# The layout of h in an fp32 decoder trunk: rows every 2048 bytes, and another layout for rows without the norm

## The chip, the core and the metric

The kernel runs on one NeuronCore of a Trainium2 chip. Its engines work side by side, each on its own stream of instructions: TensorE (PE: matmuls, and PEld, the weight loads that overlap them), VectorE (DVE), ScalarE (ACT), GpSimd (POOL) and SyncE (SP, which issues the DMAs). SBUF is the on-chip memory, 128 partitions wide; matmuls add up in the eight banks of PSUM. The metric is the device time of one execution in microseconds (us).

## What is computed

A trunk of two layers over 256 tokens and a width of 2048, all in float32. Layer 0 mixes tokens by retention, layer 1 by a short gated convolution; each is followed by a SwiGLU feed-forward of width 5632. A conditioning vector gives every sub-layer a shift, a scale and a gate.

```python
c_act = jax.nn.silu(c)
for i in range(DEPTH):
    mod = (c_act @ w_mod[i] + b_mod[i])[:, None, :]
    sh1, sc1, g1, sh2, sc2, g2 = jnp.split(mod, 6, axis=-1)
    h = (rms_norm(x, norm1_g[i]) * (1.0 + sc1) + sh1).astype(x.dtype)
    ...
    x = (x + g1 * y).astype(x.dtype)
    h = (rms_norm(x, norm2_g[i]) * (1.0 + sc2) + sh2).astype(x.dtype)
    x = (x + g2 * swiglu(h, ffn_w_in[i], ffn_w_out[i])).astype(x.dtype)
return rms_norm(x, final_g).astype(x.dtype)
```

## The kernel before, in words

Everything is kept transposed: a tile has 128 features on the partitions and the 256 tokens along the row. The 2048 features make KT = 16 such tiles, which the document calls rows: row j of h holds the features 128 j to 128 j + 127.

Precision: a float32 number is split into a high part, rounded to the type that TensorE takes in one pass (F32R), and a low part, the rest. A product is then high x high + high x low + low x high. A row of h is therefore 512 numbers in each partition: 256 of high, then 256 of low.

Weights come from HBM in one long array in the order of their use, in pieces of 128 x 2048 (`fetch`, a DMA on SP's queue, tile `raw`). `prepare` makes `hi` (L313, ScalarE) and `lo` (L316, VectorE) out of half a piece, 128 x 1024, that is eight blocks of 128 x 128. `take` hands them out one block after another.

Three functions multiply:

- `product` (L358, L361): per block one matmul of `hi` with the 512 columns of a row (high and low at once) and one of `lo` with its first 256. In it the row streams past the weights. It serves the feed-forwards and the convolution over h (3296 blocks), and the output products over `mid` (1604) and, in the retention, over tiles of the pool `rm` (496). `mid` and `rm` tiles have the shape of a row of h, 2048 bytes, each a tile of its own.
- `packed` (L398 to L400): three matmuls of 256 columns a block; for q, k and the gate in the retention, and for the last column of an output product.
- `by_token` (L373 to L375): for values v, whose tokens are to be on the partitions: here h is the stationary operand, 128 x 128, and 512 columns of weights stream.

The order is: the start (c, x and the scale and shift of layer 0 are made, first row groups of the retention's projection, up to about 190 us), the eight heads with the retention's output product, the first feed-forward in two halves (products over h, then an output product over `mid`), the convolution (over h, then its output), the second feed-forward, the last norm.

The order of TensorE's instructions, and in the start those of VectorE and ScalarE, is written by hand. The other engines' instructions are placed by a scheduler when their operands are ready.

Between two sub-layers TensorE would have to wait for the norm, a sum over all of x. The kernel avoids this: while the output product still finishes its columns, `scaled_only` (L487 to L494) writes x times the scale, without norm and without shift, into the rows of h. `normed` (L496) then multiplies these rows with the first six columns of the next weights (the first group, six PSUM banks), while the norm is worked out beside it. The norm is a factor for each token, so it can be applied to the result. The shift is not: it is multiplied as two tokens more, `ends`, whose high and low parts stand in front of a row's high part, so that two of its three matmuls take 258 columns (L519, L521) and one takes 256 (L520). Behind row k of these, `more` writes the finished rows of h (`modulated`: L465, L472, L473), at most up to row k - 1. All further groups read the finished rows.

The pools follow each other in memory: constants, work tiles, the weights' `raw`, `hi` and `lo`, then `hpool` with h, then what the retention and later the feed-forwards use (`rm`, `mid` and more). The tile `aside` of LEFT = 8 numbers stands in front of h. Row j of h begins MARGIN = 32 numbers behind the start of a stretch of 544 numbers; the two tokens of the shift are the last two of the margin.

## Time and profile before

| | before |
|---|---|
| median of 3 runs (lowest to highest) | 2639.91 us (2639.05 to 2640.29) |
| the profiled execution: its time, its span | 2639.47 us, 2637.7 us |
| mean granted TensorE clock in it | 0.998 |
| read from HBM | 682.99 MB, 260 GB/s over the span |
| DMA of the weights, w_all | 456 x 1024 KB |

How to read the lines of the profile that follow. In a group of instructions stand the source line, the engine, the operation, output<-inputs by the program's names, partitions x elements, the count, the busy time in us, the mean duration of one in ns, and the engine's idle time just before them with what ended it. A line of waits names who waited, for whom, the sum in us, how often, and the longest. In the view of one source line stand the durations (least/median/greatest, ns) and the start of the first and of the last in us. A row of stretches has the stretch, its length, the busy time and count of each engine (PE, PEld, DVE, ACT, POOL), the granted clock, the DMA engines' share and GB/s. In the timeline and in the chain of waits a row begins with its start and its length in us.

### The profile page before, as it was taken

Reading aid. Unit: us, or ns where it says so; the run is one execution under the profiler, and the core shown is the slowest. Engines: PE = TensorE matmul, PEld = TensorE weight load, DVE = VectorE, ACT = ScalarE, POOL = GpSimd, SP = SyncE. Lnnn points to the kernel's source line nnn. Section 1 sums busy time; section 2 is a strip of 40 time slices with the busy share of each in tenths; the row PEclk is TensorE's granted clock in tenths of the full one; section 3 lists DMA queues with packets and bytes.
Section 4 is the critical chain, followed back from the end, with each engine's and each line's share of the span. In section 5 each row is a group of like instructions: output and inputs, shape, how many; then the busy total and the mean of one; then the engine's idle time right before and its main releaser. Section 6 shows DMA issues by size and latency. Waiting matters only on the chain.

```text
span 2637.7 us, 38238 instructions
## 1 busy us (share of the span) xinstructions
PE 2604.2 (99%) x15220; PEld 2299.1 (87%) x15220; DVE 1989.0 (75%) x2527; ACT 1249.3 (47%) x1788; POOL 151.3 (6%) x230
## 2 busy tenths in 40 slices
PE   7999999999999999999999999999999999999998
PEld 5888889888899888888888898888988888888887
DVE  7898878777698877777777888888886665555564
ACT  5544443444456444344444454444554443444443
POOL 0000001110000011110100001100000000000000
PEclk9999999999999999999999999999999999999999
DMA  9977668777686877777777768777777665555553
GB/s 399 386 276 256 244 246 302 273 264 275 237 309 249 314 280 276 273 285 287 280 267 283 271 228 319 284 279 263 256 273 265 248 220 191 192 191 184 186 190 128
DMA packets 96950, 687.58 MB, mean 261 GB/s; under 512 B 10753, under 2 KB 12545, under 8 KB 13825
## 3 DMA queue, kind: packets, MB, share of 16 engines
q1 hardware_dynamic: 96770, 685.13, 70.8%
q8 instruction: 119, 1.95, 0.3%
q14 instruction: 61, 0.50, 0.1%
HBM read 682.99 MB, written 2.10 MB: 260 GB/s over the span
## 4 chain that ended last, share of the span: by engine, by line
PE 75%; issue 20%; DVE 2%; DMA 2%; ACT 1%; POOL 0%; DVEq 0%; ACTq 0%; POOLq 0%
PE bank L358 34%; PE bank L361 18%; PE bank L374 4%; PE bank L375 4%; PE bank L373 4%; PE bank L400 2%; PE bank L398 2%; PE bank L399 2%; PE bank L519 1%; PE bank L521 1%; PE bank L520 1%; DMA raw<-w_mod 1%; DVE raw L647 1%; DMA raw<-w_all 1%; DVE lo L316 1%
## 5 line engine op out<-in xcount | busy, mean ns | idle before, releaser
L316 DVE TENSOR_TENSOR lo<-raw,hi 128x1024 fp32r<-128x1024 f32 x912 | 1111.8, 1223 | 543.9 <-ACT hi L313 541.2
L313 ACT CAST hi<-raw 128x1024 fp32r<-128x1024 f32 x912 | 953.2, 1050 | 1073.9 <-PE bank L358 623.2
L358 PE MATMUL bank<-h,hi 128*128 128x512 f32 x3296 | 1153.8, 394 | 0.0
L361 PE MATMUL bank<-h,lo 128*128 128x256 f32 x3296 | 926.4, 281 | 0.0
L358 PEld LDWEIGHTS bank<-h,hi 128*128 128x128 f32 x3296 | 617.9, 187 | 140.0
L361 PEld LDWEIGHTS bank<-h,lo 128*128 128x128 f32 x3296 | 624.5, 189 | 0.0
L358 PE MATMUL bank<-mid,hi 128*128 128x512 f32 x1604 | 556.3, 390 | 0.0
L361 PE MATMUL bank<-mid,lo 128*128 128x256 f32 x1604 | 452.5, 282 | 1.1 <-DVE lo L316 1.1
L247 DVE SCALAR_TENSOR_TENSOR raw<-raw,cb 128x2048 f32<-128x2048 f32 x160 | 365.5, 2285 | 21.4 <-DMA raw<-w_mod 20.9
L358 PEld LDWEIGHTS bank<-mid,hi 128*128 128x128 f32 x1604 | 301.1, 188 | 63.0
L361 PEld LDWEIGHTS bank<-mid,lo 128*128 128x128 f32 x1604 | 303.4, 189 | 1.5 <-DVE lo L316 1.5
L374 PE MATMUL bank<-lo,h 128*128 128x512 f32 x512 | 203.3, 397 | 0.2 <-DVE lo L316 0.2
L373 PE MATMUL bank<-hi,h 128*128 128x512 f32 x512 | 203.4, 397 | 0.0
L375 PE MATMUL bank<-hi,h 128*128 128x512 f32 x512 | 203.2, 397 | 0.0
L358 PE MATMUL bank<-rm,hi 128*128 128x512 f32 x496 | 172.5, 391 | 0.0
L400 PE MATMUL bank<-h,lo 128*128 128x256 f32 x512 | 144.9, 283 | 9.2 <-DVE lo L316 9.2
L398 PE MATMUL bank<-h,hi 128*128 128x256 f32 x512 | 144.7, 283 | 2.5 <-ACT h L675 2.5
L399 PE MATMUL bank<-h,hi 128*128 128x256 f32 x512 | 144.4, 282 | 0.5 <-DVE h L676 0.5
L361 PE MATMUL bank<-rm,lo 128*128 128x256 f32 x496 | 139.9, 282 | 0.0
L375 PEld LDWEIGHTS bank<-hi,h 128*128 128x128 f32 x512 | 96.6, 189 | 23.3
L374 PEld LDWEIGHTS bank<-lo,h 128*128 128x128 f32 x512 | 96.5, 189 | 20.7 <-DVE lo L316 0.6
L373 PEld LDWEIGHTS bank<-hi,h 128*128 128x128 f32 x512 | 96.6, 189 | 20.2
(154 smaller groups left out, 2242.1 us busy)
## 6 DMA issues: line engine op xcount, KB each, us to landing
raw<-w_all SPq DMA_DIRECT2D x456, 1024.0 KB, 4.8
raw<-w_mod SPq DMA_DIRECT2D x192, 1024.0 KB, 5.0
x<-x_in SPq DMA_DIRECT2D x4, 512.0 KB, 5.6
out<-out SPq DMA_DIRECT2D x5, 256.0 KB, 3.4
decay<-tab_in SPq DMA_DIRECT2D x8, 128.0 KB, 2.2
out<-out SPq DMA_DIRECT2D x3, 128.0 KB, 2.5
out<-out SPq DMA_DIRECT2D x1, 384.0 KB, 2.7
cols<-cols_in SPq DMA_DIRECT2D x1, 160.0 KB, 8.7
```

Source lines behind the costliest of these rows:

```text
L247: nc.vector.scalar_tensor_tensor(raw, raw, 1.0, cb, op0=ALU.mult, op1=ALU.mult, accum_out=total)
L313: nc.scalar.copy(hi, raw)
L316: nc.vector.tensor_tensor(lo, raw, hi.bitcast(F32), op=ALU.subtract)
L358: nc.tensor.matmul(pt, hi, h, start=fresh and k == g.ks[0], stop=False, skip_group_check=True)
L361: nc.tensor.matmul(pt[:, 1, :], lo, h[:, 0, :], start=False, stop=last and k == g.ks[-1], skip_group_check=True)
L373: nc.tensor.matmul(o, ht[:, 0, :], hi, start=first, stop=False)
L374: nc.tensor.matmul(o, ht[:, 0, :], lo, start=False, stop=False)
L375: nc.tensor.matmul(o, ht[:, 1, :], hi, start=False, stop=last)
L398: nc.tensor.matmul(pt, hi, h[:, 0, :], start=first, stop=False, skip_group_check=True)
L399: nc.tensor.matmul(pt, hi, h[:, 1, :], start=False, stop=False, skip_group_check=True)
L400: nc.tensor.matmul(pt, lo, h[:, 0, :], start=False, stop=last, skip_group_check=True)
L519: nc.tensor.matmul(pt, hi, high, start=k == 0, stop=False, skip_group_check=True)
```

## The change

The margin goes. h becomes one stretch of 16 x 514 numbers, and two layouts are laid over it. The finished row j is the numbers 512 j to 512 j + 511 (`h`). The row without the norm is the numbers 514 j to 514 j + 513 (`raw_all`): first the two tokens of the shift, then 256 of high, then 256 of low. `scaled_only` and the matmuls of `normed` use the second, all else the first. A tile `beside` of 96 numbers, which nothing uses, is taken behind h. What lies behind it begins 1536 bytes lower than before. Line numbers from L485 on move by up to two.

```diff
-LEFT, MARGIN = 8, 32
+LEFT, ENDS = 8, 2
...
     hpool.tile([P, LEFT], F32, tag="aside", name="aside")
-    h_all = hpool.tile([P, KT, MARGIN + 2 * S], F32R, tag="h", name="h")
-    h = [h_all[:, j, MARGIN:].rearrange("p (a b) -> p a b", a=2) for j in range(KT)]
+    h_all = hpool.tile([P, KT * (ENDS + 2 * S)], F32R, tag="h", name="h")
+    hpool.tile([P, P - KT * ENDS], F32, tag="beside", name="beside")
+    h = [h_all[:, 2 * S * j : 2 * S * (j + 1)].rearrange("p (a b) -> p a b", a=2) for j in range(KT)]
+    raw_all = h_all.rearrange("p (k n) -> p k n", k=KT)
 
     def scaled_only(layer, norm, j):
 
         needed(layer, SC2 if norm else SC1, j)
         a = mod_a[layer][norm][:, j : j + 1]
-        nc.scalar.activation(h[j][:, 0, :], x[j], AF.Identity, scale=a)
-        nc.vector.scalar_tensor_tensor(
-            h[j][:, 1, :], x[j], a, h[j][:, 0, :].bitcast(F32), op0=ALU.mult, op1=ALU.subtract
-        )
+        high, low = raw_all[:, j, ENDS : ENDS + S], raw_all[:, j, ENDS + S :]
+        nc.scalar.activation(high, x[j], AF.Identity, scale=a)
+        nc.vector.scalar_tensor_tensor(low, x[j], a, high.bitcast(F32), op0=ALU.mult, op1=ALU.subtract)
...
-        ends = [h_all[:, :, MARGIN - 2 + i : MARGIN - 1 + i] for i in range(2)]
+        ends = [raw_all[:, :, i : i + 1] for i in range(ENDS)]
...
-            high, low = h_all[:, k, MARGIN - 2 : MARGIN + S], h[k][:, 1, :]
+            high, low = raw_all[:, k, : ENDS + S], raw_all[:, k, ENDS + S :]
```

## The prediction

> **What bounds the kernel now.** I read the page first: busy shares, then the groups of instructions.

> ```profile
> PE 2604.2 (99%) x15220; PEld 2299.1 (87%) x15220; DVE 1989.0 (75%) x2527; ACT 1249.3 (47%) x1788; POOL 151.3 (6%) x230
> ...
> L358 PE MATMUL bank<-h,hi 128*128 128x512 f32 x3296 | 1153.8, 394 | 0.0
> L361 PE MATMUL bank<-h,lo 128*128 128x256 f32 x3296 | 926.4, 281 | 0.0
> ...
> L358 PE MATMUL bank<-mid,hi 128*128 128x512 f32 x1604 | 556.3, 390 | 0.0
> ```

> TensorE is busy for 99% of the span. [...] Next I read who TensorE waited for after the first 190 us:

> ```profile
> PE bank L361 <- DVE lo L316: 1.1, 1, 1.1
> PE bank L455 <- POOL rs L448: 1.0, 1, 1.0
> PE bank L434 <- ACT acc L422: 0.9, 1, 0.9
> PE bank L874 <- DVE sp L416: 0.5, 1, 0.5
> PE bank L874 <- ACT sp L415: 0.3, 1, 0.3
> PE bank L374 <- DVE lo L316: 0.2, 1, 0.2
> ```

> That is 4 us in 2448 us. So the end is set by how fast TensorE takes its own stream, and a change of data layout matters only if it changes that pace. I therefore read the pace of the same code, `product`, from the view of one source line (count, durations, first and last start), in two stretches where it reads h and two where it reads mid:

> ```profile
> L358 PE MATMUL bank<-h,hi x704: 389/392/402, 1155.9 to 1401.9; 128*128 128x512 f32 x176
> ...
> L358 PE MATMUL bank<-h,hi x703: 390/392/402, 2255.5 to 2501.2; 128*128 128x512 f32 x176
> ...
> L358 PE MATMUL bank<-mid,hi x349: 389/390/391, 1034.2 to 1154.9; 128*128 128x512 f32 x175
> ...
> L358 PE MATMUL bank<-mid,hi x330: 389/390/394, 2501.9 to 2615.9; 128*128 128x512 f32 x165
> ```

> One block is a 512-column matmul and a 256-column one. With h it takes 246.0/703 = 349.9 and 245.7/702 = 350.0 ns; with mid 120.7/348 = 346.8 and 114.0/329 = 346.5 ns. The page says the same: 1153.8/3296 = 350.1 against 556.3/1604 = 346.8. The instructions and the weights' buffers are the same; what differs is where the moving rows lie. In the built program mid's rows follow each other every 2048 bytes, all 384 bytes past a multiple of 512. h's rows come every 2176 bytes, so each lies 128 bytes further within 512 than the one before, and the fourth comes round. The timeline of one such column shows that period (start, duration):

> ```profile
> 1284.34 0.40 PE L358 MATMUL bank<-h,hi 128*128 128x512 f32 x1
> ...
> 1284.70 0.39 PE L358 MATMUL bank<-h,hi 128*128 128x512 f32 x1
> ...
> 1285.74 0.40 PE L358 MATMUL bank<-h,hi 128*128 128x512 f32 x1
> ...
> 1287.14 0.40 PE L358 MATMUL bank<-h,hi 128*128 128x512 f32 x1
> ```

> The long one returns after 1.40 us, which is four blocks of 350 ns, and never with mid, whose longest is 391 or 394 ns.

> **The change part by part.** (1) *product over h.* After it h's rows come every 2048 bytes from byte 117632 of a partition, which is 384 past a multiple of 512: mid's places exactly. mid, rm and all that is allocated behind h move down by 1536 bytes, three times 512, and keep theirs. So I price the 3296 blocks at mid's pace: 3296 x (350.0 - 346.7) = 10.9 us off. Bounds: 346.8 and 346.5 give 10.5 and 11.5; zero if the row's place is not the cause.

> [...]

> (2) *packed over h* (L398 to L400, three 256-column matmuls a block). It runs over h in the retention stage and, on other tiles, at the ends of the output products:

> ```profile
> L398 PE MATMUL bank<-h,hi x63: 279/280/283, 433.2 to 455.2; 128*128 128x256 f32 x63
> ...
> L398 PE MATMUL bank<-mid,hi x15: 277/280/281, 1880.0 to 1884.9; 128*128 128x256 f32 x15
> ```

> 22.0/62 = 355 against 4.9/14 = 350 ns a block, and 512 blocks over h make 2.6 us. Of them 216 run in the first 190 us, where some of it is lost in waits for lo:

> ```profile
> PE bank L400 <- DVE lo L316: 7.6, 5, 2.2
> ```

> I take 2.2 us off, bounds 0 and 2.6.

> (3) *by_token* (L373 to L375). h is the stationary side here, the weights move. Six matmuls use one row of h, then six the next:

> ```profile
> L374 PE MATMUL bank<-lo,h x32: 392/395/397, 576.7 to 598.4; 128*128 128x512 f32 x32
> ```

> 21.7/31 = 700 ns for three, 233 each. Nothing in the trace has these operands on unshifted rows. The nearest from below is the six 512-column matmuls of retention, whose tiles all lie in steps of 512, read off the chain of waits:

> ```profile
> 223.13 1.37 PE bank L874 x6
> ```

> That is 685 ns for three. Between 0 and 512 x 15 ns = 7.7 us; I take 1.5, near the row of its own line, since within one row of h six matmuls already run unshifted and still take 233 each.

> (4) *normed.* Its rows now stand every 2056 bytes, with the shift's two tokens in front of the 256 of high and low behind. The place within 512 moves by 8 bytes a row, no more by 128, but odd rows start 8 bytes off a multiple of 16, and low always lies 8 bytes from high, as before.

> ```profile
> L519 PE MATMUL bank<-h,hi x72: 278/281/363, 795.4 to 820.7; 128*128 128x258 f32 x72
> ```

> 25.3/71 = 356 ns for three, 864 matmuls in all. At the pace of (2) on mid, 350 ns, it would be 288 x 6 = 1.7 us less; as a loss I allow as much. I take 0.

> (5) *Writers.* Sixteen rows each time are written by L491 and L492, now at 8-byte offsets, and by L472 and L473:

> ```profile
> L491 ACT ACTIVATE h<-x,a x48: 492/495/504, 726.2 to 1886.6; 128x256 fp32r<-128x256 f32 x48
> ```

> If misplacement doubled it, ScalarE would be busy 24 us more over three output stages; ScalarE is 47% busy and VectorE 75%, and TensorE waited for neither there. Cost 0; without that cover at most those 24 us. h[j] now overlaps the raw rows j-1 and j; but it is written only behind the matmuls of row j+1 (the last row behind its own), so no new wait ends last.

> (6) *One move in the order.* The built program differs in one place: L505 and L506, the shift's two tokens for the conv layer's norm, stood at 1313.3 us, inside the first feed-forward's second half.

> ```profile
> L505 ACT CAST h<-s x1: 219/219/219, 1313.3 to 1313.3; 128x16 fp32r<-128x16 f32 x1
> ```

> They now share bytes with rows still in use, and come behind the last product over h, at about 1402 us, behind an eviction that waits for that same product. Queued behind L505 on ScalarE is a hi cast, later by 0.22 us. They are wanted only when the conv's `normed` begins, after an output product of 352 blocks (some 120 us). Cost 0. No DMA is added or moved.

> Sum: 10.9 + 2.2 + 1.5 = 14.6 us, against the profiled execution's 2639.5 us (2637.7 of span, 1.8 around it), which is 0.4 under the median of the runs shown: **2625 us**.

> **The rivals.** *No change.* The pace may belong to the stage: over h every 16 blocks end in an eviction, over mid every 22, and the casts for SwiGLU run beside. Against it:

> ```profile
> 1200.00:1380.00 180.00, 180.00 (x1031) 158.18 (x1030) 134.04 (x160) 86.77 (x131) 12.59 (x15) 1.00 0.76 282
> 2260.00:2500.00 240.00, 240.00 (x1374) 210.75 (x1373) 135.15 (x171) 114.59 (x172) 0.00 (x0) 1.00 0.53 189
> 1040.00:1150.00 110.00, 110.00 (x636) 97.55 (x635) 81.86 (x89) 41.39 (x40) 12.82 (x19) 1.00 0.78 284
> ```

> VectorE is busy 74%, 56% and 74% in these stretches and DMA 0.76, 0.53 and 0.78: the second h stretch is much calmer and still takes 350, and the mid stretch is loaded like the first and takes 347. Time 2639.5. [...] Chance 11%.

> *Slower.* The rows of h may all land on the slow place. The slow one in four of today's takes up to 402 ns against mid's 390, 12 ns more; if each row did so, a block would take 346.7 + 12 = 358.7 and 3296 of them 28.7 us more: 2668. It would decide from the first product behind `normed`, near 821 us. For it: the long matmul does fall on some place, and one fixed place could be that. Against: mid's rows sit on the very place that h's get. Chance 5%.

> *Gain taken back.* A faster TensorE uses up its weights sooner and waits for lo, so half the gain goes: 2632. Against: in mid's stretches it runs at 347 with VectorE 74% busy, and the waits quoted show 1.1 us in one place. Chance 6%.

> **How the numbers follow.** Forecast 78%, no change 11%, gain taken back 6%, slower 5%. The forecast's own bounds are 10.5 + 0 + 0 - 1.7 = 8.8 us off (2631) and 11.5 + 2.6 + 7.7 + 1.7 = 23.5 us off (2616); the two further cases outside hold 16%, so the range is 2616 to 2632, which reaches the third. A measurement of this kernel tells 0.2%, 5.3 us, from no change: faster 0.83, same 0.12, slower 0.05.

> **What would show it.** Right: the line view of L358 over h shows 346.7 ns from start to start and no duration over 394; L358 over mid is unmoved; about 11 us go between 821 and 2501 us, and little before 190. L398 at 350 and L374 between 685 and 700 a block would show (2) and (3). Wrong: L358 over h still at 350, or at a new pace above it; L519's three over 362; or a new wait of TensorE for lo or h. Were mid's pace to change as well, the place within 512 bytes would not be what counts.

## The result, and the profile after

| | before | after |
|---|---|---|
| median of 6 runs each (lowest to highest), us | 2639.79 (2639.05 to 2640.29) | 2629.99 (2627.28 to 2632.28) |
| ratio of the times, 95% interval | | 0.9962 (0.9949 to 0.9975) |
| the profiled execution: its time, its span, us | 2639.47, 2637.7 | 2630.33, 2628.6 |
| mean granted clock in it | 0.998 | 0.996 |

The change makes the kernel 9.8 us faster, 0.38%. The forecast was 2625 us in a range of 2616 to 2632: the time lies in the range, 5 us over the forecast.

The first lines that answer are those of the page of the kernel after (share of the span, then count, busy time, mean duration):

```profile
PE 2596.0 (99%) x15220; PEld 2301.1 (88%) x15220; DVE 1988.8 (76%) x2527; ACT 1249.2 (48%) x1788; POOL 149.8 (6%) x230
...
L358 PE MATMUL bank<-h,hi 128*128 128x512 f32 x3296 | 1142.8, 390 | 0.0
L361 PE MATMUL bank<-h,lo 128*128 128x256 f32 x3296 | 929.5, 282 | 0.0
...
L358 PE MATMUL bank<-mid,hi 128*128 128x512 f32 x1604 | 556.3, 390 | 0.0
```

The group over h went from 1153.8 to 1142.8 us, with the same count; the group over mid stayed at 556.3. A block over h now takes 1142.8/3296 = 346.7 ns on the page, as over mid. (The two matmuls of a block last 390 and 282 ns by the records, 672 together, so these lie over each other, and a pace is taken from one start to the next.) The view of line L358 by stretches (least, median and greatest duration, then the first and the last start) shows that it does so in each stage:

```profile
L358 PE MATMUL bank<-mid,hi x352: 390/390/390, 1032.9 to 1154.6; 128*128 128x512 f32 x176
...
L358 PE MATMUL bank<-h,hi x704: 390/390/390, 1154.9 to 1398.6; 128*128 128x512 f32 x176
...
L358 PE MATMUL bank<-h,hi x703: 390/390/390, 2248.4 to 2491.7; 128*128 128x512 f32 x176
...
L358 PE MATMUL bank<-mid,hi x330: 390/390/390, 2492.4 to 2606.5; 128*128 128x512 f32 x165
```

243.7/703 = 346.7 and 243.3/702 = 346.6 ns from start to start over h, and no duration but 390: the long matmul of 402 ns is gone, not rarer. The waits of TensorE after the first 190 us are those of before, with no new one:

```profile
PE bank L455 <- POOL rs L448: 1.0, 1, 1.0
PE bank L434 <- ACT acc L422: 0.9, 1, 0.9
PE bank L361 <- DVE lo L316: 0.9, 1, 0.9
PE bank L876 <- DVE sp L416: 0.5, 1, 0.5
PE bank L876 <- ACT sp L415: 0.3, 1, 0.3
```

And in the stretches of the prediction's table TensorE starts more matmuls in the same time (1041 for 1031, 1386 for 1374), beside as much work of the others and the same share of DMA:

```profile
1200.00:1380.00 180.00, 180.00 (x1041) 159.59 (x1040) 134.62 (x161) 86.86 (x131) 12.62 (x15) 1.00 0.75 281
...
2260.00:2500.00 240.00, 240.00 (x1386) 212.75 (x1385) 137.28 (x174) 115.75 (x173) 0.00 (x0) 1.00 0.53 190
```

**Where the time went, along the clock.** Lay the starts of the same instruction side by side in the two profiled executions. The first stretch of product over h that the prediction shows began at 1155.9 and now begins at 1154.9 us; it ended at 1401.9, now 1398.6. The last one went from 2255.5 to 2248.4 and from 2501.2 to 2491.7; the last product over mid from 2615.9 to 2606.5. So the lead grows from 1.0 to 3.3 us inside one stage over h, from 7.1 to 9.5 inside the other, and does not grow over mid. But it should have been 2 us at 1155 already for the 608 blocks of the first stage alone, and more for `packed`. It started from a loss, which the last of the start's `by_token` shows (the view of L375 up to 185 us, first before, then after):

```profile
L375 PE MATMUL bank<-hi,h x106: 392/396/628, 23.6 to 183.1; 128*128 128x512 f32 x106
```

```profile
L375 PE MATMUL bank<-hi,h x106: 387/397/632, 23.8 to 184.7; 128*128 128x512 f32 x106
```

The kernel after is 1.6 us late there. The table of stretches shows why this can be so (the third number from the end is the granted clock; first before, then after):

```profile
51.40:54.80 3.40, 3.40 (x13) 2.92 (x12) 2.00 (x2) 3.40 (x8) 0.00 (x0) 0.51 1.02 422
```

```profile
27.10:30.50 3.40, 3.40 (x13) 3.15 (x14) 3.40 (x3) 1.80 (x3) 0.00 (x0) 0.50 1.01 422
...
51.00:54.40 3.40, 3.40 (x13) 2.81 (x11) 2.36 (x2) 3.40 (x7) 0.00 (x0) 0.50 1.02 422
156.80:160.20 3.40, 3.40 (x12) 2.84 (x12) 3.40 (x4) 0.95 (x2) 0.00 (x0) 0.50 0.88 371
```

For some 3.4 us at a time the clock was granted at half (0.51 in the row of before, 0.50 in the three of after). Before had one such stretch in the start, after had three. A matmul of 512 columns lasts 628 or 632 ns in it instead of 396. Two stretches more cost at most 2 x 1.7 = 3.4 us, half of their length, which is an estimate from these rows. Two kernels of the experiments below bear it out. They read the same finished rows and differ from the kernel after in the layout of the rows without the norm, which are first written at some 727 us. One (low in front) has a single such stretch in its start, the other (old pitch) has two. The same `by_token` matmul, the first of its run near 190 us, begins at 188.8, 190.3 and 191.9 us with one, two and three stretches (low in front, old pitch, after):

```profile
L373 PE MATMUL bank<-hi,h x31: 393/396/397, 188.8 to 209.8; 128*128 128x512 f32 x31
```

```profile
L373 PE MATMUL bank<-hi,h x32: 393/396/396, 190.3 to 212.0; 128*128 128x512 f32 x32
```

```profile
L373 PE MATMUL bank<-hi,h x31: 393/395/396, 191.9 to 212.9; 128*128 128x512 f32 x31
```

So in these three traces each stretch more goes with a start some 1.5 us later. The six runs of the kernel after, at mean clocks of 0.996 to 0.998, lie 5.0 us apart. The two at 0.998 are the fastest, but the slowest is at 0.997, so the clock is not all of it.

### The profile page after: what moved, and what is told of

It is laid out like the page before. It is cut to its first block, busy times and chain, and to the rows that moved or that the text cites. A ratio compares the mean times of both kernels' runs of the same rounds, so it can differ in the third digit from the quotient of the medians.

```text
span 2628.6 us, 38238 instructions
## 1 busy us (share of the span) xinstructions
PE 2596.0 (99%) x15220; PEld 2301.1 (88%) x15220; DVE 1988.8 (76%) x2527; ACT 1249.2 (48%) x1788; POOL 149.8 (6%) x230
## 4 chain that ended last, share of the span: by engine, by line
PE 76%; issue 20%; DVE 2%; DMA 1%; ACT 1%; POOL 0%; DVEq 0%; ACTq 0%; POOLq 0%
PE bank L358 34%; PE bank L361 18%; PE bank L373 4%; PE bank L374 4%; PE bank L375 4%; PE bank L400 2%; PE bank L398 2%; PE bank L399 2%; PE bank L521 1%; PE bank L523 1%; PE bank L522 1%; DVE raw L649 1%; DMA raw<-w_all 1%; DVE lo L316 1%; PE bank L876 1%
## 5 line engine op out<-in xcount | busy, mean ns | idle before, releaser
L316 DVE TENSOR_TENSOR lo<-raw,hi 128x1024 fp32r<-128x1024 f32 x912 | 1111.8, 1222 | 537.5 <-ACT hi L313 533.3
L358 PE MATMUL bank<-h,hi 128*128 128x512 f32 x3296 | 1142.8, 390 | 0.0
L361 PE MATMUL bank<-h,lo 128*128 128x256 f32 x3296 | 929.5, 282 | 0.0
L358 PEld LDWEIGHTS bank<-h,hi 128*128 128x128 f32 x3296 | 618.4, 188 | 129.5
L361 PEld LDWEIGHTS bank<-h,lo 128*128 128x128 f32 x3296 | 622.9, 189 | 0.0
L358 PE MATMUL bank<-mid,hi 128*128 128x512 f32 x1604 | 556.3, 390 | 0.0
L361 PE MATMUL bank<-mid,lo 128*128 128x256 f32 x1604 | 452.4, 282 | 0.9 <-DVE lo L316 0.9
L358 PEld LDWEIGHTS bank<-mid,hi 128*128 128x128 f32 x1604 | 300.9, 188 | 63.1
L361 PEld LDWEIGHTS bank<-mid,lo 128*128 128x128 f32 x1604 | 303.1, 189 | 1.2 <-DVE lo L316 1.2
L373 PE MATMUL bank<-hi,h 128*128 128x512 f32 x512 | 204.4, 399 | 0.0
L374 PE MATMUL bank<-lo,h 128*128 128x512 f32 x512 | 203.8, 398 | 0.0
L375 PE MATMUL bank<-hi,h 128*128 128x512 f32 x512 | 203.6, 398 | 0.0
L358 PE MATMUL bank<-rm,hi 128*128 128x512 f32 x496 | 172.5, 390 | 0.0
L400 PE MATMUL bank<-h,lo 128*128 128x256 f32 x512 | 144.6, 282 | 8.3 <-DVE lo L316 8.3
L398 PE MATMUL bank<-h,hi 128*128 128x256 f32 x512 | 145.0, 283 | 2.5 <-ACT h L677 2.5
L361 PE MATMUL bank<-rm,lo 128*128 128x256 f32 x496 | 139.8, 282 | 0.0
L375 PEld LDWEIGHTS bank<-hi,h 128*128 128x128 f32 x512 | 97.0, 189 | 23.5
L373 PEld LDWEIGHTS bank<-hi,h 128*128 128x128 f32 x512 | 97.0, 189 | 20.2
L374 PEld LDWEIGHTS bank<-lo,h 128*128 128x128 f32 x512 | 97.0, 189 | 20.1
```

The costliest lines, as they stand in the source:

```text
L316: nc.vector.tensor_tensor(lo, raw, hi.bitcast(F32), op=ALU.subtract)
L358: nc.tensor.matmul(pt, hi, h, start=fresh and k == g.ks[0], stop=False, skip_group_check=True)
L361: nc.tensor.matmul(pt[:, 1, :], lo, h[:, 0, :], start=False, stop=last and k == g.ks[-1], skip_group_check=True)
L373: nc.tensor.matmul(o, ht[:, 0, :], hi, start=first, stop=False)
L374: nc.tensor.matmul(o, ht[:, 0, :], lo, start=False, stop=False)
L375: nc.tensor.matmul(o, ht[:, 1, :], hi, start=False, stop=last)
```

## The experiments

All times stand beside a run of the kernel before on the same chip. One run each, except the last; single runs of the kernel after differ by up to 5 us, so the verdicts rest on the paces in the traces, which repeat to a tenth of a nanosecond from stage to stage (over h 349.99 to 350.00 in the five stages before, 346.67 in each of the five after), and not on the last microseconds of a time. "Place" means the number of bytes past a multiple of 512 in a partition, taken from the addresses of the built program: in the kernel before, `hi` and `lo` stand at 352, `mid` at 384, h at 0, 128, 256, 384 in turn; after, h at 384. "Pace" is ns per block, start to start: for `product` one 512-column and one 256-column matmul, for `packed` and `by_token` three. Paces without a view beside them are worked out from the starts in the trace, gaps left out.

### Does the step from row to row count?

**The step halved.** The kernel before with rows every 2112 bytes, 64 further each time.

```diff
-LEFT, MARGIN = 8, 32
+LEFT, MARGIN = 8, 16
```

> The layout of before with a margin of 64 bytes in place of 128, so that a row of h begins 64 bytes further within 512 than the one before it. Theory (each round of 512 bytes that the rows drift through costs TensorE a fixed stretch, 13.3 ns by before's 350.0 against 346.7 ns over four rows): eight rows to a round, so a block of product over h takes 346.7 + 13.3/8 = 348.3 ns, and the time is about 5.5 us under before's 2639.8. Rival one (any step that is not a whole 512 costs the same): 350.0 ns, 2639.8. Rival two (only rows that begin on a multiple of 128 are fast): over 350 ns for the half of the rows that do not, time over 2639.8. Blocks over mid stay at 346.7 in all three.

Measured: 2645.07 us, before 2638.97. Line view of L358 in two stages:

```profile
L358 PE MATMUL bank<-h,hi x605: 393/397/399, 823.4 to 1035.8; 128*128 128x512 f32 x152
...
L358 PE MATMUL bank<-h,hi x703: 391/393/398, 1159.2 to 1404.9; 128*128 128x512 f32 x176
```

212.4/604 = 351.7 ns in the stages behind `normed`, 245.7/702 = 350.0 in those behind a product over mid, which stays at 346.7. A step of 64 bytes comes round every 8 rows and is no cheaper. So the price did not hang on how often the place passes a multiple of 512, which I had taken for the cause of one long matmul in four. And one layout has two paces, by the stage it is entered from.

**The step turned round.** The kernel before, with row j in stretch 15 - j (the shift's tokens are put in the same order).

```diff
...
-    h = [h_all[:, j, MARGIN:].rearrange("p (a b) -> p a b", a=2) for j in range(KT)]
+    h = [h_all[:, KT - 1 - j, MARGIN:].rearrange("p (a b) -> p a b", a=2) for j in range(KT)]
...
```

> The layout of before with row j of h in slot 15 - j, so that the rows taken one after the other lie 128 bytes back within 512, not on. Theory (a drift forwards makes TensorE lose 13.3 ns per round of 512 bytes): a drift backwards costs nothing or gives it back, 343.3 to 346.7 ns a block over h, time 2617 to 2629. Rival (what costs is that neighbouring rows differ, in either direction): 350.0 ns and 2639.8.

Measured: 2637.92 us, before 2638.97. The page:

```profile
L359 PE MATMUL bank<-h,hi 128*128 128x512 f32 x3296 | 1153.8, 393 | 0.0
```

1153.8 us, as before to the digit. The direction did not matter.

**The same rows in another order.** The kernel before, with the rows put into the 16 stretches so that most steps are a multiple of 512 bytes (stretches 0, 4, 8, 12, 1, 5, ... one after the other), and in a second kernel a multiple of 256 (0, 2, ..., 14, 1, 3, ..., 15). All 16 stretches are used as often as before; only the sequence differs.

```diff
+SLOT = [[0, 4, 8, 12, 1, 5, 9, 13, 2, 6, 10, 14, 3, 7, 11, 15].index(j) for j in range(KT)]
...
+    h = [h_all[:, SLOT[j], MARGIN:].rearrange("p (a b) -> p a b", a=2) for j in range(KT)]
...
```

```diff
+SLOT = [[0, 8, 1, 9, 2, 10, 3, 11, 4, 12, 5, 13, 6, 14, 7, 15].index(j) for j in range(KT)]
...
```

> The layout of before (rows every 2176 bytes), but row j of h in the slots 0, 4, 8, 12, 1, 5, 9, 13, 2, ... so that 12 of 16 steps from row to row are whole multiples of 512 bytes and 4 of 16 are 128 bytes on. Theory (what counts is the place within 512 bytes against the last row's): three quarters of the loss go, 346.7 + 3.3/4 = 347.5 ns a block over h, 3296 x 2.5 ns = 8 us less, about 2631.5. Rival (it is the distance of 2048 bytes itself, or the stretch without gaps): 350.0 ns and 2639.

> The layout of before, row j of h in the slots 0, 2, 4, ... 14, 1, 3, ...: nearly every step from row to row is 256 bytes within 512. Theory with a period of 512 bytes: as with 64 and 128 bytes, 350 ns a block or a little more, time 2639 to 2645. Rival with a period of 256 bytes: 346.7 + a sixteenth of the two odd steps, about 347.1 ns, time 2630.

Measured: 2637.26 and 2630.11 us, before 2639.73. The pages, first of the order by 512, then by 256:

```profile
L360 PE MATMUL bank<-h,hi 128*128 128x512 f32 x3296 | 1148.4, 392 | 0.0
```

```profile
L360 PE MATMUL bank<-h,hi 128*128 128x512 f32 x3296 | 1145.6, 392 | 0.0
```

Against 1142.8 us after, a column of 16 blocks costs (1148.4 - 1142.8) x 16/3296 = 27 ns more in the one, 2.8 x 16/3296 = 14 in the other, and 11.0 x 16/3296 = 53 before. (Of the 5.4 us that this gives the order by 512, its time shows 2.5: TensorE loses 1.9 us in waits for weights in one group of `by_token`, 456 to 480 us.) The order by 512 has four steps in a column that are an odd multiple of 128 bytes, the order by 256 has two, the kernel before sixteen. A timeline of the order by 512 shows its long ones (0.40) eight blocks apart, two in a column:

```profile
1284.97 0.40 PE L360 MATMUL bank<-h,hi 128*128 128x512 f32 x1
...
1287.76 0.40 PE L360 MATMUL bank<-h,hi 128*128 128x512 f32 x1
...
1290.55 0.40 PE L360 MATMUL bank<-h,hi 128*128 128x512 f32 x1
```

So two odd steps cost some 13.5 ns where they stand apart (14 ns for two, 27 for four); when each of the sixteen is odd, the column costs 53 ns, four times 13.3 and not eight times. The fourteen steps of 256 bytes in the second order add nothing that shows to the 14 ns of its two odd ones. So in these kernels the place counts within 256 bytes, not 512, and the cost goes with the change of place.

### Does any constant place do?

**All rows at 0.** The kernel after with 128 bytes more in front of h; mid and rm move along, the weights stay at 352.

```diff
-LEFT, ENDS = 8, 2
+LEFT, ENDS = 40, 2
```

> The changed kernel with 128 bytes more in front of h: h, mid and all behind them begin at 0 within 512 bytes in place of 384; the rows still follow every 2048 bytes. Theory (it is the constancy from row to row that counts): blocks over h and over mid stay at 346.7 ns, time that of the changed kernel, 2627 to 2632. Rival (384 is a good place of its own, mid having had it by luck or choice): both paces go up, towards 350 or more, 3 ns on 5396 blocks being 16 us, 2646.

Measured: 2628.33 us, before 2638.97. Product over h, mid and rm at 346.7, all as in the kernel after; `packed` in the second pair of heads 352.0 instead of 350.0.

**The weights moved.** The kernel after with the 32 bytes in front of h taken ahead of the weights' pools instead: `hi` and `lo` at 384 like h, which stays.

```diff
+    pad = ctx.enter_context(tc.tile_pool(name="pad", bufs=1))
+    pad.tile([P, LEFT], F32, tag="aside", name="aside")
...
-    hpool.tile([P, LEFT], F32, tag="aside", name="aside")
```

> The changed kernel with the 32 bytes that stood in front of h moved in front of the weights' buffers: hi and lo then begin at 384 within 512 bytes, as h, mid and the retention's tiles do, in place of 352; h and all behind it stay. Theory for by_token (it runs at 233 ns a matmul since its moving weights and its stationary h lie on places that differ): its three matmuls go from 700 towards the 685 of L876, 512 x 15 ns = up to 7.7 us less. Rival (233 ns is the pace of 512 columns after 512 columns, wherever they lie): 700 stays, time 2627 to 2632. Blocks over h and mid: 346.7 by both.

Measured: 2627.62 us, before 2639.73. Product over h and mid at 346.7, but over rm, whose rows lie at 384 too, at 353.3; `packed` 360.0; `by_token` faster for the first time:

```profile
L376 PE MATMUL bank<-lo,h x32: 389/389/397, 645.6 to 666.7; 128*128 128x512 f32 x32
```

21.1/31 = 681 ns for three, where every kernel so far had 699 or 700.

Three more kernels, each made from the kernel after, move the two places apart. In the first and the third a pad stands ahead of the weights (24 and 16 numbers) and the space in front of h makes up for it: h stays at 384 (512 bytes further on), and the weights go to 448 and to 416. In the second the weights stay at 352, and h, mid and rm go to 448.

```diff
-LEFT, ENDS = 8, 2
+LEFT, ENDS = 112, 2
...
+    pad = ctx.enter_context(tc.tile_pool(name="pad", bufs=1))
+    pad.tile([P, 24], F32, tag="pad", name="pad")
```

```diff
-LEFT, ENDS = 8, 2
+LEFT, ENDS = 24, 2
```

```diff
-LEFT, ENDS = 8, 2
+LEFT, ENDS = 120, 2
...
+    pad = ctx.enter_context(tc.tile_pool(name="pad", bufs=1))
+    pad.tile([P, 16], F32, tag="pad", name="pad")
```

> The changed kernel with hi and lo at 448 within 512 bytes (352 in the changed kernel, 384 in e7_weights384), h and all behind it still at 384. In e7 by_token went from 700 to 681 ns for three, packed over h from 350 to 360 and product over rm from 346.4 to 353. Theory one (by_token gains when the moving side begins on a multiple of 64 bytes; packed and product lose when weights and rows have the same place): by_token 681, packed 350, product 346.7, time some 10 us under the changed kernel's 2627 to 2632. Theory two (both come from weights and h having the same place): by_token back at 700, packed 350, rm 346.4, time as the changed kernel's.

> The changed kernel with h, mid and all behind them 64 bytes further: 448 within 512 bytes, the weights left at 352, so that the rows lie 96 bytes on from the weights' place (32 in the changed kernel, 160 in e2_place0, 0 in e7, 64 back in e9). Theory one (a pair of places in step costs 353.3 ns a block where they differ by 64 bytes in one direction, and e9 has met that case alone): 346.7 ns over h and mid, time 2627 to 2632. Theory two (rows and weights must differ by less than 64 bytes or by a multiple of 128 of the changed kernel's 32): over 350, up to 353.3 ns and 2650 to 2661.

> The changed kernel with hi and lo at 416 within 512 bytes and h and all behind it at 384: the weights lie 32 bytes behind the rows' place, not 32 before it. Theory one (what counts is which of the two is ahead, as e9 had the weights ahead by 64): some 350 to 353 ns a block, 2640 to 2660. Theory two (32 bytes apart either way is good): 346.7 ns, 2627 to 2632.

Measured: 2660.71 us (before 2637.91), 2651.64 and 2666.07 (before 2641.18). Line views of one stage over h, in this order:

```profile
L360 PE MATMUL bank<-h,hi x700: 397/397/398, 1158.7 to 1405.7; 128*128 128x512 f32 x175
```

```profile
L358 PE MATMUL bank<-h,hi x703: 392/394/394, 1163.2 to 1408.9; 128*128 128x512 f32 x176
```

```profile
L360 PE MATMUL bank<-h,hi x703: 395/401/401, 1165.9 to 1413.9; 128*128 128x512 f32 x176
```

247.0/699 = 353.4, 245.7/702 = 350.0 and 248.0/702 = 353.3 ns, and mid the same in each. All three have rows at a constant place. So a constant place is not enough: its place against the weights' counts as well. Over rm, with the weights at 416, the pace even changes between pieces of the same product. Its views up to 352.5 us, up to 361.5 and from 362 on give

```profile
L360 PE MATMUL bank<-rm,hi x24: 392/392/397, 342.5 to 351.2; 128*128 128x512 f32 x24
...
L360 PE MATMUL bank<-rm,hi x24: 392/392/402, 352.9 to 361.0; 128*128 128x512 f32 x24
...
L360 PE MATMUL bank<-rm,hi x208: 392/396/476, 362.2 to 435.4; 128*128 128x512 f32 x104
```

Blocks that follow each other without a gap take 347 ns in the first 24 and 353 in the next 24 and all after; six matmuls of another kind stand between. All six places, in ns a block:

| weights | rows | weights - rows | product over h and mid | over rm |
|---|---|---|---|---|
| 352 | 384 (after) | -32 | 346.7 | 346.7 |
| 352 | 0 (as 512) | -160 | 346.7 | 346.7 |
| 384 | 384 | 0 | 346.7 | 353.3 |
| 416 | 384 | +32 | 353.3 | 347, then 353.3 |
| 448 | 384 | +64 | 353.3 | 353.3 |
| 352 | 448 | -96 | 350.0 | 350.0 |

In these last three kernels `packed` takes 353, 360 and 355 ns in the second pair of heads (weights at 448, rows at 448, weights at 416), and `by_token` 687 with a few groups at 700, 703, and 700. Both theories for the weights at 448 had 346.7 and missed. The weights at 416 came out as slow as theory one had it, by which weights ahead of the rows are slow; but with the rows at 448 the rows are ahead, by 96, and 350.0 is slow too. So these runs give no rule for which pair is fast.

### What do the raw rows cost?

**Low in front.** The kernel after with a row without the norm laid out as low, the two tokens, high.

```diff
-        high, low = raw_all[:, j, ENDS : ENDS + S], raw_all[:, j, ENDS + S :]
+        high, low = raw_all[:, j, ENDS + S :], raw_all[:, j, :S]
...
```

> The changed kernel with the low part of a row without the norm put first, then the shift's two tokens and high: the three matmuls of normed then begin at the same place within 512 bytes (low and high 1024 bytes apart), not 8 bytes apart. Theory (TensorE loses time where one matmul's start differs from the last one's within 512 bytes): the three take some 352 ns (3 x 116.7 and two columns more in two of them) in place of 360 now and 356 in before, 288 x 8 = 2.3 us less than the changed kernel. Rival (it is the odd 8 bytes that cost): still 360 ns. The blocks of product over h stay at 346.7 ns in both.

**Their old pitch.** The kernel after, with the finished rows every 2048 bytes, and the rows without the norm every 2176 again.

```diff
...
-    h_all = hpool.tile([P, KT * (ENDS + 2 * S)], F32R, tag="h", name="h")
-    hpool.tile([P, P - KT * ENDS], F32, tag="beside", name="beside")
+    h_all = hpool.tile([P, KT * (MARGIN + 2 * S)], F32R, tag="h", name="h")
...
-    raw_all = h_all.rearrange("p (k n) -> p k n", k=KT)
+    raw_all = h_all.rearrange("p (k n) -> p k n", k=KT)[:, :, MARGIN - ENDS :]
```

> The changed kernel with the rows without the norm back at 2176 bytes (before's margin of 128), the finished rows every 2048 from the same start. Theory (normed lost time because its rows now begin on odd multiples of 8 bytes): its three matmuls go from 360 back to before's 356 ns, 288 x 4 = 1.2 us less than the changed kernel, blocks over h 346.7. Rival (the finished rows' new place makes normed slower by what modulated writes into them meanwhile): 360 stays.

Measured: 2626.86 us (before 2638.97) and 2627.60 (before 2639.73). Start to start, `normed` takes 359.4 ns for three matmuls after, 358.3 with low in front, and 355.1 at the old pitch, as before; the rest is as in the kernel after. So it is the pitch of 2056 bytes that costs 4 ns a block; which half stands in front changes 1 ns of it.

### Both together

The kernel after with the weights at 384 and the old pitch of the raw rows: the faster `by_token` of the one, the `normed` of the other.

```diff
...
+    pad = ctx.enter_context(tc.tile_pool(name="pad", bufs=1))
+    pad.tile([P, LEFT], F32, tag="aside", name="aside")
...
-    hpool.tile([P, LEFT], F32, tag="aside", name="aside")
...
-    raw_all = h_all.rearrange("p (k n) -> p k n", k=KT)
+    raw_all = h_all.rearrange("p (k n) -> p k n", k=KT)[:, :, MARGIN - ENDS :]
```

> e7_weights384 and e8_rawpitch together: weights, h and all behind it at 384 within 512 bytes, finished rows every 2048 bytes, rows without the norm every 2176. If the paces add up as they stood alone: by_token 681 ns (512 x 19 ns = 9.8 us less than the changed kernel), packed over h 360 (512 x 10 = 5.1 us more), product over rm 353 (496 x 6.6 = 3.3 us more), normed 356 in place of 360 (1.2 us less): 2.6 us under the changed kernel's 2630, about 2627, and 12.5 us under before. Rival (normed's new pitch throws packed or product over h into another pace, as the places of weights and rows do): over 347 ns over h, and a time at or over the changed kernel's.

Measured, in five runs: 2657.78 us (2655.98 to 2659.23), before 2640.28; ratio 1.0066 (1.0052 to 1.0079). Slower than before, although each half alone was faster. Its line view:

```profile
L360 PE MATMUL bank<-h,hi x701: 395/398/403, 1158.5 to 1405.8; 128*128 128x512 f32 x176
...
L360 PE MATMUL bank<-mid,hi x80: 395/398/403, 1805.0 to 1832.9; 128*128 128x512 f32 x80
...
L360 PE MATMUL bank<-mid,hi x159: 390/391/397, 1833.9 to 1888.7; 128*128 128x512 f32 x159
```

247.3/700 = 353.3 ns over h, where the same places gave 346.7 with the other raw rows. And in the third output product the pace changes in the middle: 27.9/79 = 353.2 ns up to 1833 us, 54.8/158 = 346.8 from there on. Between the two lies one wait of TensorE for weights (its weight loads in the timeline):

```profile
1833.11 0.19 PEld L360 LDWEIGHTS bank<-mid,hi 128*128 128x128 f32 x1
1833.69 0.19 PEld L363 LDWEIGHTS bank<-mid,lo 128*128 128x128 f32 x1 [0.39 <-DVE lo L318]
```

Same matmuls, same places; at a gap of 0.39 us the stream goes from one pace into the other, and it stays there until the next stage. The kernel with the weights at 384 alone bears this out. Its rows over rm, h and mid all lie at 384, and it has both paces, 353.3 over rm and 346.7 over h and mid. In its third output product the same wait comes (0.56 us, at 1816 us), and here are the views of L360 before and behind it:

```profile
L360 PE MATMUL bank<-mid,hi x80: 392/394/395, 1787.3 to 1814.7; 128*128 128x512 f32 x80
...
L360 PE MATMUL bank<-mid,hi x157: 391/391/391, 1816.9 to 1871.0; 128*128 128x512 f32 x157
```

Blocks take 344 and 350 ns by turns in the first and 347 each in the second: the pattern changes at the wait, and only the mean stays. In the kernel with the weights at 448 the same wait comes and the pace stays at 353. With the places of the kernel after, the wait comes too (0.9 us at L361, above), and 346.7 stands on both sides of it. So two pairs of places were seen at two steady paces: weights and rows at 384 (346.7 and 353.3 ns), and over rm the weights at 416 with rows at 384 (347 and 353). The pace changed at the start of a stage, behind six other matmuls or at the wait of 0.39 us; what picks the one or the other was not shown. With the weights at 352 and rows at 384 only the fast one was seen, in every stage of the eight kernels in which such rows are read (mid in the one before and its four variants, mid and h in the one after and in the two with other raw rows).

## Why the prediction came out as it did

**(1) product over h, -10.9 us: right in mechanism and size.** The page shows -11.0 (1153.8 to 1142.8). The reason given, that h's place moves from row to row, holds: the order by 256 bytes, in which the same 16 stretches of memory are read in another sequence, takes 8.2 of the 11.0 us. Its period was wrong by a factor of two (256, not 512), which does no harm here since 2048 is a multiple of both. What made the size safe was the other half of the reason: h gets mid's own place against the same weights. "A constant place" alone would not have carried it (353.4, 353.3 and 350.0 ns over h in three of the kernels with one).

**(2) packed over h, -2.2 us: right in kind, several times too large.** The pace fell as forecast in the stretch from which it was read, the second pair of heads. The view of L398, before and after:

```profile
L398 PE MATMUL bank<-h,hi x64: 279/280/283, 432.9 to 455.2; 128*128 128x256 f32 x64
```

```profile
L398 PE MATMUL bank<-h,hi x64: 277/279/280, 434.4 to 456.4; 128*128 128x256 f32 x64
```

22.3 and 22.0 us for 63 steps; the paces are 355 and 350 ns. But the forecast took this stretch for all 512 blocks. In the four other long ones outside the start (558 to 648 us) the kernel before had 352.3 to 352.5 ns, and the kernel after has 350.0 in three and 353.4 in one. Laid side by side, all `packed` over h outside the start gives 0.4 us, not the 1.5 of 296 blocks at 5 ns. What the start's 216 gave can't be seen under its loss.

**(3) by_token, -1.5 us: wrong, it is 0.** After, in the view of L374:

```profile
L374 PE MATMUL bank<-lo,h x32: 395/396/397, 577.4 to 599.1; 128*128 128x512 f32 x32
```

21.7/31 = 700 ns, unchanged. The bound of 0 was the value to take: here h is loaded as weights and `hi` and `lo` move, and it was mostly moving those that changed the pace, to 681 at 384 (moving h to 448 made it 703).

**(4) normed, 0 within 1.7: it is a loss of 1.2 us.**

```profile
L521 PE MATMUL bank<-h,hi x72: 278/282/364, 796.2 to 821.8; 128*128 128x258 f32 x72
```

25.6/71 = 360.6 ns against 356.3 (one long step in each), times 288 blocks. The old pitch takes it back, as the kernel with it shows. A step of 2056 bytes changes the place with each row, by 8.

**(5) and (6), 0: nothing seen.** The writers' 495 ns are 496 now, and the moved cast stands where it was expected, with nothing behind it late:

```profile
L495 ACT ACTIVATE h<-x,a x48: 492/496/500, 726.7 to 1881.2; 128x256 fp32r<-128x256 f32 x48
...
L507 ACT CAST h<-s x1: 222/222/222, 1400.3 to 1400.3; 128x16 fp32r<-128x16 f32 x1
```

**The sum.** Between 190 us and the end of the last output product the kernel after gains 11.0 us by the starts of the same matmuls. The parts come to 10.9: 11.0 from (1) and 0.4 from (2), less 1.2 by (4), and 0.7 from two waits for lo that it does not meet or meets shorter (in `by_token` near 461 us, and over mid). With the start 1.6 us late and 0.3 us lost behind the last product, the profiled execution is 9.1 us faster. So of the forecast's 14.6 us, (2) was 1.8 too large, (3) 1.5 and (4) 1.2, and the start and the end took 1.9 that it had no term for; the two waits, which it did not foresee either, gave 0.7 back. The range held because its slow bound had put (2) and (3) at nothing and (4) at a loss; the forecast itself leant to the fast side in all three. The fastest run of the kernel after, 2627.28, lies 11.8 us under the fastest before. The prediction had no term for the start's half-clock stretches. That the change caused the two more was not shown: across the kernels of this study, the start has one such stretch in six, two in seven, and three in the kernel after alone, and the kernels with all of h's finished rows where the change puts them have one, two or three.

**The rivals.** "No change" fell with the first line: the pace belongs to the rows, not to the stage. The rows' place is not all of it: the pace went from 346.7 to 353.3 ns when the weights' buffers moved by 64 bytes, from 352 to 416, with the rows left at 384, so where the weights lie tells on the stream too. The casts that write the weights moved along, but the pace does not hang on whether one is running: with the weights at 448, between 1170 and 1395 us, the 553 blocks with a cast running beside them and the 83 without one all take 353 or 354 ns. "Slower" did not come about, but its mechanism is real: a poor constant place was worth 353.3 ns, not the 358.7 assumed, and 2660 to 2666 us, with mid at that pace too. What it hung on was the place against the weights. "Gain taken back" fell with the waits: 0.9 us for lo, in one place, as before.

## What to carry to other kernels

When one form of instruction runs at two paces in one trace, compare what it reads, address by address: the slower group's rows drifted by 128 bytes, and giving them the places of the faster group was worth just the difference (350.1 to 346.7 ns a block on the pages, 11.0 us). Copy a place that the trace shows to be fast, against the same weights; don't reason that any even place will do, for of the five other ones tried three were slower (353.3 ns a block over h twice, 350.0 once), and a fourth (weights and rows at 384) took 346.7 ns over h in one kernel and 353.3 in another. Two edits that each gain may lose together, so the combination has to be run: of the kernels here that beat the one before, none was shown by its time to beat the kernel after, whose own runs reach from 2627 to 2632 (2626.86 with low in front, 2627.60 with the old pitch of the raw rows, one run each). Between 190 us and the last output product, where no half-clock stretch falls, one trace each gives 2425.8 us before, 2414.8 after, 2413.9 with the old pitch and 2413.2 with the weights at 384.
